# Input projection of a hybrid decoder layer: split weights are kept in DRAM by the second block of tokens and loaded by later ones

## The chip, the cores and the metric

The kernel runs on one core of a Trainium2 chip. The metric is the time of one execution on the device in microseconds, as the median of several runs. A core has a matmul engine (TensorE, PE in the profile; its weight loads are PEld), a vector engine (VectorE, DVE), a scalar engine (ScalarE, ACT), GpSimd (POOL) and a sync engine (SyncE, SP) that here issues every DMA. Each engine works through its own queue of instructions in a fixed order; a semaphore wait at the head of a queue holds all that stands behind it.

## The reference, cut to what matters

One decoder layer over 2048 tokens of width 1024, in float32. The change lies in the first line of it, the combined input projection `h @ w_in` with its 2832 columns:

```python
h = rmsnorm(x, norm_mix[l])
proj = h @ w_in[l]
a_q, a_f, a_i, a_g, b_x, b_g, c_q, c_k, c_v, c_g, c_lr = jnp.split(proj, IN_SPLITS, axis=-1)
o_a = hgrn2_mixer(a_q, a_f, a_i, a_g, lb[l], hgrn_norm[l])
o_b = rglru_mixer(b_x, b_g, ...)
o_c = gla_mixer(c_q, c_k, c_v, c_g, c_lr, ...)
x = x + jnp.concatenate([o_a, o_b, o_c], axis=-1) @ w_out[l]
...                                   # gated MLP with a width-3 convolution, final norm
```

## The kernel before

**Two-part products.** A float32 product is made of three matmuls: every operand is split into a high part (rounded to the matmul's own format, float32r) and a low part (the rest), and `mm3` (L134) adds high x high, high x low and low x high. `split` (L110) makes both parts: a copy into the high part (L106 on ACT, L108 on DVE) and a subtraction into the low part (L113). For weights this is done in `load_w` (L115): a load of raw weights into a tile `wr` (pool `wraw`, three buffers), then the split into `wh` and `wl` (pool `wsp`, three buffers of each), 128 partitions x up to 1024 columns. A table `W_SPLIT` (L38) says for each kind of weights which engine makes which part, and how far ahead of its place the split is put in the order:

```python
W_SPLIT = {"z": ("vector", "vector", 320), "cv": ("scalar", "vector", 0), "qk": ("vector", "vector", 20),
           "ai": ("scalar", "vector", 80), "g": ("scalar", "vector", 160), "bg": ("scalar", "vector", 320),
           "bi": ("vector", "gpsimd", 320), ...}
```

**Blocks of tokens.** The tokens are worked on in four blocks of 512 (`b` = 0 to 3). For each block `in_steps` (L243) lists the steps of the projection for the head groups A and C: two columns blocks `z`, the value weights `cv` (three tiles of weights that all four 128-token steps use) , four `qk`, the `ai` weights (two tiles), four `g`. One column block is `proj` (L185): `load_w`, then 8 x 3 = 24 matmuls of 512 columns. Weights are loaded and split anew for every block. The projection of block `b + 1` is merged, step by step, with the mixing of block `b` (`mix_steps`, L347), which is many small instructions on DVE, ACT, POOL and PE; this is set out at L694 to L712.

**B columns.** For the last block the eight columns blocks of head group B (`s_bg`, L333, kind `bg`) are projected beside its mixing, and the results go to DRAM (`bg_d`). For blocks 0 to 2 the same eight column blocks are projected later, in the B stage (`b_in`, L740, kind `bi`), from `hT`, the turned and split activations, that were kept in DRAM (`h_d`). There each block's `b_in` stands ahead of its `b_mix` (the gated recurrence, mostly DVE) and of `b_out` of the block before (the output projection, with loads of `xr` and stores to `x2_d`). The first `b_in` is put in the order beside the last block's mixing.

**Order.** A scheduler at build time orders each engine's instructions by their place in the program, shifted by `high_priority`, and by when their inputs are expected; buffers are given out as they come free. After about 960 us only the MLP is left, which the change doesn't touch.

Of the kernel before, what the change touches and what calls it, by code (L numbers as in the profile page):

```python
# [8 lines left out]
F32 = mybir.dt.float32  # L9
F32R = mybir.dt.float32r  # L10
I32 = mybir.dt.int32
AF = mybir.ActivationFunctionType
# [4 lines left out]
P = 128  # L17
D = 1024
KT = D // P
# [14 lines left out]
A_Q, A_F, A_I, A_G, B_X, B_G, C_Q, C_K, C_V, C_G, C_LR = (  # L34
    0, 256, 512, 768, 1024, 1536, 2048, 2176, 2304, 2560, 2816)
# [9 lines left out]
def kernel(ctx: ExitStack, tc: tile.TileContext, x, norm_mix, w_in, hgrn_lower_bounds, hgrn_norm,  # L45
# [4 lines left out]
    vec, act, pool, pe, sync = nc.vector, nc.scalar, nc.gpsimd, nc.tensor, nc.sync  # L50
    x, out, w_in, w_out = x[0], out[0], w_in[0], w_out[0]
# [4 lines left out]
    def pool_at(stack, nbytes, name, bufs, **kw):  # L56

        stack.enter_context(tc.tile_pool(name="pad_" + name, bufs=1, **kw)).tile([P, nbytes // 4], F32, name="pad")
        return stack.enter_context(tc.tile_pool(name=name, bufs=bufs, **kw))
# [3 lines left out]
    wsp = pool_at(ctx, 320, "wsp", 3)  # L63
# [5 lines left out]
    dram = ctx.enter_context(tc.tile_pool(name="dram", bufs=1, space=DRAM))  # L69
# [16 lines left out]
    def mm_bank():  # L86
        return bank("mm", 4)

    def aux_bank():
        return bank("aux", 2)  # L90
# [13 lines left out]
    def copy(eng, o, i):  # L104
        if eng is act:
            act.activation(o, i, AF.Copy)  # L106
        else:
            eng.tensor_copy(o, i)  # L108

    def split(raw, hi, lo, e_hi=act, e_lo=vec):  # L110

        copy(e_hi, hi, raw)
        e_lo.tensor_tensor(lo, raw, hi.bitcast(F32), op=ALU.subtract)  # L113

    def load_w(src, n1, n2, tag, tail=None, wpool=None, wcols=D):  # L115

        def part(pool_, dt, nm):
            return pool_.tile([P, wcols], dt, name=nm, tag=nm)[:, :n1 * n2].rearrange("p (a b) -> p a b", b=n2)
        hl = [part(wpool or wsp, F32R, "wh"), part(wpool or wsp, F32R, "wl")]
        raw = part(wraw, F32, "wr")  # L120
        if tail is None:
            sync.dma_start(out=raw, in_=src)
        else:
            m = src.shape[-1]
            sync.dma_start(out=raw[:, :, :m], in_=src)
            sync.dma_start(out=raw[:, :, m:], in_=tail)
        e_hi, e_lo, ahead = W_SPLIT[tag]
        with tc.high_priority(offset=ahead):
            split(raw, hl[0], hl[1], getattr(nc, e_hi), getattr(nc, e_lo))
        return hl  # L130

    w_in_v = w_in.rearrange("(kt p) c -> p kt c", p=P)
# [46 lines left out]
    def proj_mm(w, hT):  # L179
        o = mm_bank()  # L180
        for kt in range(KT):
            mm3(o, [a[:, kt, :] for a in w], [a[:, kt, :] for a in hT], kt == 0, kt == KT - 1)
        return o

    def proj(hT, col, tag):  # L185

        return proj_mm(load_w(w_in_v[:, :, col:col + P], KT, P, tag), hT)

    def merged(a, b):

# [38 lines left out]
    with ExitStack() as cx:  # L229
# [13 lines left out]
        def in_steps(b, B):  # L243
            steps = []
            blk = blks[b % 2]


            def s_z(c):
                if c == 0:
                    B["K"] = blk.tile([P, 3, TB], F32, name="K")  # L250
                    B["L"] = blk.tile([P, 3, TB], F32, name="L")
                copy(vec, B["K"][:, c, :], proj(B["hT"], A_F + c * P, "z"))
            for c in range(2):
                steps.append(lambda c=c: s_z(c))


            def s_vw(col, n):
                if n > 256:
                    B["V"] = blk.tile([P, NTK, 528], F32, name="V")
                B["kn"] = 3 if n > 256 else 4  # L260
                B["ws"] = []
                for k0 in range(0, KT, B["kn"]):
                    ks = slice(k0, min(k0 + B["kn"], KT))
                    B["ws"].append(load_w(w_in_v[:, ks, col:col + 256], ks.stop - k0, n, "cv" if n > 256 else "ai",
                                          w_in_v[:, ks, C_LR:C_LR + 16] if n > 256 else None))

            def s_v(n, at, t):
                o = mm_bank()
                for kt in range(KT):
                    mm3(o[:, :n], [a[:, kt, t * P:(t + 1) * P] for a in B["hT"]],  # L270
                        [a[:, kt % B["kn"], :] for a in B["ws"][kt // B["kn"]]], kt == 0, kt == KT - 1)
                copy(vec, B["V"][:, t, at:at + n], o[:, :n])

            def s_gate():
                V, K, L = B["V"], B["K"], B["L"]
                lr = tmp.tile([16, TB], F32, name="lr", tag="X")
                pt = aux_bank()
                for t in range(NTK):  # L280
                    pe.transpose(out=pt[:16, t * P:(t + 1) * P], in_=V[:, t, 512:528], identity=ident)
                vec.tensor_copy(lr, pt[:16, :])
                gl = aux_bank()
                pe.matmul(gl, gup, lr, start=True, stop=True)
                e, u1 = t2(), t2()
                f = tmp.tile([P, 2, TB], F32, name="f", tag="f", bufs=1)
                z, l01, mn = K[:, 0:2, :], L[:, 0:2, :], L[:, 2, :]
                act.activation(e, gl, AF.Abs, bias=pc["bg"])
                act.activation(e, e, AF.Exp, scale=-1.0)
                act.activation(f, z, AF.Sigmoid)  # L290
                act.activation(z, z, AF.Sigmoid, scale=-1.0)
                vec.tensor_scalar(mn, gl, pc["bg"], 0.0, op0=ALU.add, op1=ALU.min)
                vec.tensor_scalar(u1, e, 1.0, None, op0=ALU.add)
                vec.scalar_tensor_tensor(e, u1, -1.0, e, op0=ALU.add, op1=ALU.subtract)
                for c in range(2):
                    vec.tensor_scalar(f[:, c, :], f[:, c, :], lb1[:, c:c + 1], lb[:, c:c + 1],
                                      op0=ALU.mult, op1=ALU.add)
                vec.tensor_scalar(l01, f, LN_MIN, None, op0=ALU.max)
                vec.tensor_scalar(f, f, F_FLOOR, LN_MIN, op0=ALU.max, op1=ALU.min)
                act.activation(u1, u1, AF.Ln)  # L300
                act.activation(l01, l01, AF.Ln)
                act.activation(f, f, AF.Ln, scale=LN_UP)
                if run.get("out"):
                    run.pop("out")()
                vec.tensor_tensor(e, e, u1, op=ALU.subtract)
                vec.tensor_tensor(mn, mn, e, op=ALU.add)
                vec.tensor_scalar(mn, mn, 1.0 / 16.0, None, op0=ALU.mult)
                vec.scalar_tensor_tensor(l01, f, lnc, l01, op0=ALU.subtract, op1=ALU.add)
                for c in range(2):
                    vec.tensor_scalar(K[:, c, :], K[:, c, :], lb1[:, c:c + 1], None, op0=ALU.mult)  # L310
            for t in range(NTK):
                steps.append(lambda t=t: (s_vw(C_V, 272) if t == 0 and b > 0 else None, s_v(272, 256, t)))
            steps.append(s_gate)


            def s_qk(nm, c, col, scale):
                if nm not in B:
                    B[nm] = blk.tile([P, 3, TB], F32, name=nm)
                act.activation(B[nm][:, c, :], proj(B["hT"], col, "qk"), AF.Copy, scale=scale)
            for nm, c, col, scale in (("Q", 0, A_Q, 1.0), ("Q", 1, A_Q + P, 1.0), ("Q", 2, C_Q, C_SCALE),  # L320
                                      ("K", 2, C_K, 1.0)):
                steps.append(lambda a=(nm, c, col, scale): s_qk(*a))
            for t in range(NTK):
                steps.append(lambda t=t: (s_vw(A_I, 256) if t == 0 else None, s_v(256, 0, t)))


            def s_g(k):
                g = t2()
                copy(vec, g, proj(B["hT"], (A_G, C_G)[k // 2] + (k % 2) * P, "g"))
                sync.dma_start(out=g_d[b][k], in_=g)  # L330


            def s_bg(k):  # L333
                g = t2()
                copy(act, g, proj(B["hT"], (B_X, B_G)[k % 4 // 2] + (k // 4 * 2 + k % 2) * P, "bg"))
                sync.dma_start(out=bg_d[k], in_=g)
            B["load"] = lambda: s_vw(C_V, 272)
            return (steps, [lambda k=k: s_g(k) for k in range(4)],
                    [lambda k=k: s_bg(k) for k in range(8)] if b == NB - 1 else [])

# [217 lines left out]
        for gi, group in enumerate((rows, frows)):  # L558
            n = sum(r[2] for r in group)
# [86 lines left out]
        for b in LEVELS[:5]:  # L646
            n = 64 // b
# [667 lines left out]
```

## Time and profile before

| | us |
|---|---|
| median of 3 runs | 2220.92 |
| lowest and highest | 2212.77, 2224.83 |
| profiled execution, its own time | 2215.95 |
| span of the profiled execution | 2214.2 |

The profile is one execution. Engine times are busy times, of which several can run at once. A matmul's end is modelled, so PE's busy share is an upper bound of how full it is; how dense it works is read from how far apart matmuls start. The page counts 321.41 MB moved by DMA, 145 GB/s on average, nearly all through one queue (SP's).

### The profile page before, as it was taken

The page shows a single profiled execution, that of the slowest core. Times are in us where ns is not written, and L with a number is a line of the kernel's source. Part 1 is how long each engine was busy: PE and PEld are TensorE (multiplying, and loading weights), DVE is VectorE, ACT ScalarE, POOL GpSimd, SP SyncE. Part 2 cuts the span into 40 slices and gives each one's busy share as a digit, 9 for nine tenths or more (in the row PEclk, how much of TensorE's full clock was granted, in tenths as well). Part 3 has the DMA queues.
Part 4 walks back from the last instruction along what each step waited for, and adds up shares of the span by engine and source line. Part 5 has one row for each costly group of instructions (what it writes and reads, how often), then busy time and mean ns, then how long its engine had stood idle before and what let it go on. Part 6 is the DMA issues. An engine that isn't in the chain of part 4 may idle for free.

```text
span 2214.2 us, 31440 instructions
## 1 busy us (share of the span) xinstructions
PE 2142.7 (97%) x12118; PEld 1761.8 (80%) x12118; DVE 1678.8 (76%) x2366; ACT 987.5 (45%) x1361; POOL 349.3 (16%) x456
## 2 busy tenths in 40 slices
PE   7999999999899999999999999999999999999998
PEld 6887778777667878988888887788888887888886
DVE  7799998988768778786676766666666678679676
ACT  3453535433156467454444445544444455226332
POOL 2232341516333231000000000000000000000000
PEclk9999999999999999999999999999999999999999
DMA  7352432345144736643342435522222258667653
GB/s 260 116 180 73 162 97 65 96 148 184 60 136 176 225 121 190 202 136 119 110 134 87 133 95 182 190 80 86 86 86 86 85 176 276 209 205 254 217 174 111
DMA packets 313699, 321.41 MB, mean 145 GB/s; under 512 B 17347, under 2 KB 267214, under 8 KB 312014
## 3 DMA queue, kind: packets, MB, share of 16 engines
q1 hardware_dynamic: 313550, 319.41, 44.5%
q8 instruction: 95, 1.56, 0.3%
q14 instruction: 54, 0.44, 0.1%
HBM read 233.38 MB, written 85.98 MB: 144 GB/s over the span
## 4 chain that ended last, share of the span: by engine, by line
PE 54%; DVE 7%; DMA 5%; ACT 2%; issue 2%; POOL 0%; SPq 0%; DVEq 0%; POOLq 0%; ACTq 0%
PE mm L1072 26%; PE sc L1072 13%; PE aux L1072 6%; PE sc L137 2%; PE sc L138 2%; PE sc L136 2%; DVE wl L113 1%; DMA x_d<-xr 1%; PE mm L138 1%; PE mm L136 1%; PE mm L137 1%; DMA xt<-x_d 1%; DVE xc L801 1%; DMA y<-ps_d 1%; PE mm L913 1%
## 5 line engine op out<-in xcount | busy, mean ns | idle before, releaser
L106 ACT ACTIVATE wh<-wr 128x1024 fp32r<-128x1024 f32 (+3 forms) x217 | 200.8, 928 | 354.6 <-PE mm L1072 91.2
L113 DVE TENSOR_TENSOR wl<-wr,wh 128x1024 fp32r<-128x1024 f32 (+2 forms) x241 | 260.8, 1085 | 102.5 <-ACT wh L106 98.3
L106 ACT ACTIVATE wh<-s 128x1024 fp32r<-128x1024 f32 x116 | 123.0, 1062 | 251.7 <-PE sc L1072 197.8
L138 PE MATMUL mm<-hTh,wl 128*128 128x512 f32 x576 | 231.0, 401 | 2.8 <-POOL wl L113 2.4
L136 PE MATMUL mm<-hTh,wh 128*128 128x512 f32 x576 | 233.6, 406 | 0.0
L137 PE MATMUL mm<-hTl,wh 128*128 128x512 f32 x576 | 231.7, 402 | 0.0
L404 POOL TENSOR_TENSOR qc<-Q,X 32x128 f32<-32x128 f32 x224 | 151.0, 674 | 247.3 <-ACT X L390 116.4
L1072 PE MATMUL mm<-t34h,wh 128*128 128x512 f32 x464 | 181.1, 390 | 1.3 <-DVE y L1238 0.9
L1072 PE MATMUL mm<-t34h,wl 128*128 128x512 f32 x464 | 180.6, 389 | 0.0
L1072 PE MATMUL mm<-t34l,wh 128*128 128x512 f32 x464 | 180.5, 389 | 0.0
L113 DVE TENSOR_TENSOR wl<-s,wh 128x1024 fp32r<-128x1024 f32 x116 | 141.4, 1221 | 18.5 <-ACT wh L106 18.4
L137 PE MATMUL sc<-wl,oh 128*128 128x256 f32 x512 | 146.8, 287 | 2.4 <-DVE wl L113 2.4
L136 PE MATMUL sc<-wh,oh 128*128 128x256 f32 x512 | 146.3, 287 | 0.2 <-DVE xr L834 0.2
L138 PE MATMUL sc<-wh,ol 128*128 128x256 f32 x512 | 145.4, 284 | 0.0
L138 PEld LDWEIGHTS mm<-hTh,wl 128*128 128x128 f32 x576 | 108.6, 189 | 31.1 <-issue 4.3
L136 PEld LDWEIGHTS mm<-hTh,wh 128*128 128x128 f32 x576 | 108.4, 188 | 28.9 <-issue 6.8
L137 PEld LDWEIGHTS mm<-hTl,wh 128*128 128x128 f32 x576 | 108.7, 189 | 27.8 <-issue 7.3
L1141 DVE SCALAR_TENSOR_TENSOR ga<-gr,pcol,ga 128x1024 f32<-128x1024 f32 x84 | 107.6, 1281 | 0.4 <-issue 0.3
L1072 PEld LDWEIGHTS mm<-t34h,wh 128*128 128x128 f32 x464 | 87.1, 188 | 21.2 <-issue 1.7
L137 PEld LDWEIGHTS sc<-wl,oh 128*128 128x128 f32 x512 | 97.5, 190 | 5.8 <-DVE wl L113 3.0
L1072 PEld LDWEIGHTS mm<-t34h,wl 128*128 128x128 f32 x464 | 87.1, 188 | 18.2
L1072 PEld LDWEIGHTS mm<-t34l,wh 128*128 128x128 f32 x464 | 87.1, 188 | 17.9
(335 smaller groups left out, 5508.4 us busy)
## 6 DMA issues: line engine op xcount, KB each, us to landing
wr<-in_w_in_dram SPq DMA_DIRECT2D x80, 512.0 KB
wr<-in_ffn_w_gate_dram SPq DMA_DIRECT2D x42, 512.0 KB
wr<-in_ffn_w_val_dram SPq DMA_DIRECT2D x42, 512.0 KB
wr<-in_w_out_dram SPq DMA_DIRECT2D x32, 512.0 KB
gr_d<-v SPq DMA_DIRECT2D x32, 512.0 KB
ps_d<-y SPq DMA_DIRECT2D x32, 512.0 KB
wr<-gr_d SPq DMA_DIRECT2D x32, 512.0 KB
wr<-in_ffn_w_down_dram SPq DMA_DIRECT2D x25, 512.0 KB
```

The costliest lines, as they stand in the source:

```text
L106: act.activation(o, i, AF.Copy)
L113: e_lo.tensor_tensor(lo, raw, hi.bitcast(F32), op=ALU.subtract)
L136: pe.matmul(o, lh, rh, start=first, stop=False)
L137: pe.matmul(o, lh, rl, start=False, stop=False)
L138: pe.matmul(o, ll, rh, start=False, stop=last)
L404: pool.tensor_tensor(qc[p_, h, :].rearrange("p (n s) -> p n s", s=lev), qo[p_, 2], xo[p_, 2], op=ALU.mult)
L801: vec.tensor_tensor_scan(xc[:, i, :], r[:, i, :], th[:, i, :], initial=hs0[:, c:c + 1], op0=ALU.mult, op1=ALU.add)
L913: pe.transpose(out=pt[:, k * P:(k + 1) * P], in_=xt[:, (k0 + k) * P:(k0 + k + 1) * P], identity=ident)
L1072: pe.matmul(o, lhs[a], rhs[b], start=first and k == 0 and i == 0, stop=last and k == KH - 1 and i == 2, skip_group_check=True)
L1141: vec.scalar_tensor_tensor(ga, gr[:, k:k + TH], pc[f"fw{k}"][:, f:f + 1], ga, op0=ALU.mult, op1=ALU.add)
```

## The change

`load_w` gets a key. The first call with a key that is to be kept loads and splits as before and then stores both parts to two DRAM tiles; a later call with the same key loads the two parts straight into `wh` and `wl`, without `wr` and without a split. Block 0 neither stores nor finds anything (`keep` is `b > 0`), block 1 stores all its 15 weight tiles (30 stores), blocks 2 and 3 load them (60 loads instead of 30). In the last block the eight `bg` calls store (16 stores), and the 24 `bi` calls of blocks 0 to 2 find the same columns (48 loads instead of 24). Two unused arguments go. The loads and stores of parts are issued by SP at their place in the program; the rows of a part tile in DRAM are 4 KB long for 1024 columns, those of the raw weights 512 or 1024 bytes.

```diff
-    def load_w(src, n1, n2, tag, tail=None, wpool=None, wcols=D):
+    parts_d = {}
+
+    def load_w(src, n1, n2, tag, tail=None, key=None, keep=True):
...
-        hl = [part(wpool or wsp, F32R, "wh"), part(wpool or wsp, F32R, "wl")]
+        hl = [part(wsp, F32R, "wh"), part(wsp, F32R, "wl")]
+        if key in parts_d:
+            for a, d in zip(hl, parts_d[key]):
+                sync.dma_start(out=a.bitcast(F32), in_=d)
+            return hl
         raw = part(wraw, F32, "wr")
...
             split(raw, hl[0], hl[1], getattr(nc, e_hi), getattr(nc, e_lo))
+        if key is not None and keep:
+            parts_d[key] = [dram.tile([P, n1, n2], F32, name=f"w_{tag}{len(parts_d)}_{i}") for i in range(2)]
+            for a, d in zip(hl, parts_d[key]):
+                sync.dma_start(out=d, in_=a.bitcast(F32))
         return hl
...
-    def proj(hT, col, tag):
+    def proj(hT, col, tag, keep=True):
 
-        return proj_mm(load_w(w_in_v[:, :, col:col + P], KT, P, tag), hT)
+        return proj_mm(load_w(w_in_v[:, :, col:col + P], KT, P, tag, key=col, keep=keep), hT)
...
-                copy(vec, B["K"][:, c, :], proj(B["hT"], A_F + c * P, "z"))
+                copy(vec, B["K"][:, c, :], proj(B["hT"], A_F + c * P, "z", b > 0))
...
-                                          w_in_v[:, ks, C_LR:C_LR + 16] if n > 256 else None))
+                                          w_in_v[:, ks, C_LR:C_LR + 16] if n > 256 else None, key=("v", col, k0), keep=b > 0))
...
-                act.activation(B[nm][:, c, :], proj(B["hT"], col, "qk"), AF.Copy, scale=scale)
+                act.activation(B[nm][:, c, :], proj(B["hT"], col, "qk", b > 0), AF.Copy, scale=scale)
...
-                copy(vec, g, proj(B["hT"], (A_G, C_G)[k // 2] + (k % 2) * P, "g"))
+                copy(vec, g, proj(B["hT"], (A_G, C_G)[k // 2] + (k % 2) * P, "g", b > 0))
```

## Rows read from the trace of the kernel before

**Rows 1.** The page's first part: busy time, share of the span, instructions.

```profile
PE 2142.7 (97%) x12118; PEld 1761.8 (80%) x12118; DVE 1678.8 (76%) x2366; ACT 987.5 (45%) x1361; POOL 349.3 (16%) x456
```

**Rows 2.** Table of stretches: length, busy time (instructions) of each engine, clock, DMA.

```profile
core 0: us, PE busy (x) PEld busy (x) DVE busy (x) ACT busy (x) POOL busy (x), PEclk, DMA share, GB/s
...
240.00:360.00 120.00, 113.12 (x1012) 92.58 (x1011) 114.39 (x195) 48.17 (x75) 40.18 (x58) 1.00 0.30 89
360.00:490.00 130.00, 125.80 (x1070) 99.52 (x1068) 115.35 (x201) 59.86 (x85) 38.39 (x56) 1.00 0.31 94
490.00:560.00 70.00, 65.17 (x519) 50.61 (x518) 62.98 (x90) 22.62 (x43) 44.47 (x57) 1.00 0.61 203
560.00:640.00 80.00, 75.80 (x450) 49.96 (x450) 52.95 (x88) 19.29 (x28) 23.40 (x21) 1.00 0.23 68
640.00:800.00 160.00, 149.15 (x786) 123.31 (x785) 128.24 (x129) 88.99 (x104) 60.66 (x37) 0.97 0.55 179
...
960.00:2214.00 1254.00, 1238.01 (x5495) 1020.34 (x5494) 881.90 (x1123) 542.22 (x737) 67.47 (x108) 1.00 0.44 143
```

**Rows 3.** Who waited for whom, 240 to 800 us: total, times, longest.

```profile
DVE wh L108 <- PE mm L137: 12.0, 8, 4.3
...
PE sc L427 <- DVE qa L400: 8.3, 7, 2.8
PE aux L775 <- ACT r L777: 6.0, 2, 4.6
...
PE aux L516 <- DVE hl L113: 3.0, 4, 1.2
PE mm L138 <- POOL wl L113: 2.4, 1, 2.4
```

**Rows 4.** The chain that ended last: start, duration, what; B stage, then MLP.

```profile
668.04 3.35 DVE xc L792
...
672.89 0.74 DVE xc L755
...
676.50 2.81 DVE xc L755
...
683.64 3.35 DVE th L797
...
754.04 2.41 DVE wh L108
...
756.62 4.55 DVE ol L113 x2
...
772.16 1.14 DVE th L797
...
1000.22 2.72 PE mm L1072 x12
```

**Rows 5.** Table of stretches again, two of ten microseconds.

```profile
690.00:700.00 10.00, 5.36 (x20) 3.60 (x19) 9.88 (x14) 8.51 (x11) 1.52 (x3) 0.85 0.17 52
700.00:710.00 10.00, 10.00 (x60) 8.11 (x59) 5.94 (x7) 8.71 (x10) 3.95 (x1) 0.81 0.85 341
```

**Rows 6.** DVE's groups of weight splits, 240 to 490: busy us, mean ns, idle before.

```profile
L113 DVE TENSOR_TENSOR wl<-wr,wh 128x1024 fp32r<-128x1024 f32 x25 | 31.4, 1264 | 2.8 <-ACT wh L106 2.5
...
L108 DVE CAST wh<-wr 128x1024 fp32r<-128x1024 f32 x10 | 7.1, 714 | 1.1 <-PE mm L137 0.6 <-PE mm L138 0.4
...
L113 DVE TENSOR_TENSOR wl<-wr,wh 128x816 fp32r<-128x816 f32 x2 | 2.0, 1000 | 0.0
...
L113 DVE TENSOR_TENSOR wl<-wr,wh 128x544 fp32r<-128x544 f32 x2 | 1.7, 860 | 0.0
```

**Rows 7.** GpSimd's group of weight splits, whole span.

```profile
L113 POOL TENSOR_TENSOR wl<-wr,wh 128x1024 fp32r<-128x1024 f32 x24 | 63.8, 2659 | 107.0 <-DVE wh L108 46.2 <-DMA oa<-o_ac_d 19.9 <-PE mm L138 18.4
```

**Rows 8.** SP's queue, 490 to 560 us: what it waited for.

```profile
SPq L336 <- ACT t L106: 38.3, 7, 9.8
```

**Rows 9.** A 512 KB load in 4 KB rows: SP's issue; DMA share, 294 to 298.

```profile
294.54 0.34 SPq L175 DMA_DIRECT2D wbc<-in_norm_ffn_dram  x1
...
DMA  0000000000000002954998996989963334021000
```

More of the change, by code (lines that the diff above doesn't have):

```diff
@@ L113, in split @@
         e_lo.tensor_tensor(lo, raw, hi.bitcast(F32), op=ALU.subtract)
-    def load_w(src, n1, n2, tag, tail=None, wpool=None, wcols=D):
+    parts_d = {}
+    def load_w(src, n1, n2, tag, tail=None, key=None, keep=True):
         def part(pool_, dt, nm):
-            return pool_.tile([P, wcols], dt, name=nm, tag=nm)[:, :n1 * n2].rearrange("p (a b) -> p a b", b=n2)
-        hl = [part(wpool or wsp, F32R, "wh"), part(wpool or wsp, F32R, "wl")]
+            return pool_.tile([P, D], dt, name=nm, tag=nm)[:, :n1 * n2].rearrange("p (a b) -> p a b", b=n2)
+        hl = [part(wsp, F32R, "wh"), part(wsp, F32R, "wl")]
[3 more added lines that the diff above has]
+            return hl
         raw = part(wraw, F32, "wr")
```

## The prediction

> **What bounds the kernel now.** I read the table of stretches first, then the list of who waited, then the chain of waits, then the groups of split instructions. The page says that TensorE (PE) is busy for 97% of the span [rows 1], and from 960 us to the end it really is dense: 1238 of 1254 us [rows 2], at one 512-column matmul every 2.72/12 = 0.227 us [rows 4]. The change doesn't touch that part. In the input projection the picture is less clean. From 240 to 490 us, when the projection of the third and fourth block of tokens (blocks 2 and 3) runs under the mixing of blocks 1 and 2, VectorE (DVE) is busy 114.4 + 115.3 = 229.7 of 250 us and PE 238.9 [rows 2]. Two engines are both close to full, so what one is spared can only be gained as far as the other has idle time. PE's idle time, stretch by stretch, is 6.9 and 4.2 us (240 to 490), 4.8 and 4.2 (490 to 640) and 10.9 (640 to 800), 31 us together [rows 2]. This is a lower bound of its slack: a matmul is drawn about 0.39 us long and the next starts after 0.227, so a stall under some 0.16 us isn't seen.
>
> Most of what PE waited for there by name comes out of DVE or out of the scalar engine (ACT) behind it: 8.3 us for `qa`, 6.0 for `r`, 3.0 for `hl`, and only 2.4 in the row for the weights' low part [rows 3]. So weights are not what PE lacks; DVE's time is. The chain of waits says the same from 664 to 690 us and from 752 to 785: it consists of DVE instructions end to end, and three kinds of them are stretched. Line 792 took 3.35 us and line 797 3.35 us, where line 797 took 1.14 us undisturbed; line 755 took 2.81 us against 0.74 [rows 4]. Each stretch falls on one of the 24 low-part splits that GpSimd (POOL) does for the B columns, of 2.66 us mean [rows 7].
>
> **The change part by part.**
>
> *Blocks 2 and 3 don't split (removed).* Per block: 2 `z`, 4 `qk`, 2 `ai`, 4 `g` tiles of 1024 columns and three `cv` tiles. On DVE that is, for two blocks, 24 low parts at 1.264 us = 30.3, 12 high parts at 0.714 = 8.6, 4 x 1.000 and 2 x 0.860 for `cv`, in all 44.6 us of its 229.7 [rows 6, 2] (the stretch cuts a little off at either end, so its groups count 25 and 10 instead of 24 and 12). ACT loses 18 high parts too, but at 108 of 250 us [rows 2] it isn't a bound. With 185 us left, DVE falls well below PE; what is late next is PE itself, whose idle time there is 11.1 us [rows 2]. I take 7 us of it; the ends are 0 (PE's order stays as full of small switches as now) and 17 (the unseen stalls go too).
>
> *B columns of blocks 0 to 2 don't split (removed).* 24 high parts on DVE and 24 low parts on POOL, 63.8 us of POOL [rows 7]. Between 490 and 640 us the high parts also hold DVE up, since they stand in its queue and wait for PE to free a weight slot, 12.0 us in 8 waits, the longest 4.3 [rows 3]; the mixing of the last block queues behind them. PE's idle time in this stretch is 9.0 us [rows 2]; I take 4 (0 to 9). From 640 to 800 us I go by the chain: four stretched pieces (668.04, 676.50, 683.64, 756.62) give back 2.2 + 2.1 + 2.2 + 2.3 = 8.8 us (the last, two instructions of 1024 columns, against twice 1.14), the high part at 754.04 goes with 2.4, and six further high parts at some 0.6 with 3.6; together 14.8 us [rows 4]. PE comes next there: 10.9 us idle [rows 2], and it ran at a granted clock of 0.85 and 0.81 of full (part of the time at 1.2 instead of 2.4 GHz) in the ten microseconds in which it was idle for 4.6 us and in the ten behind them [rows 5]. I take 10 (4 to 16).
>
> The Trainium skill, SBUF — State Buffer, section "SBUF: two separate sides", has a rule for the stretched rows: a DVE instruction with two SBUF inputs and a GpSimd instruction hold a shared port pair in turn, each for its whole length. The trace agrees where the two meet (3.35 instead of 1.14 us). By the rule alone up to 24 x 2.66 = 64 us of DVE's time could come back, by the rows the 8.8 us that lay on the chain; I keep the rows, because PE caps it.
>
> *Loads (added).* 30 loads of raw weights in blocks 2 and 3 become 60 part loads, 24 for the B columns become 48. The nearest row is a 512 KB load in 4 KB rows: issued at 294.54, its packets end 3.1 us later, and the digits of the 16 engines' share add up to about 1.3 us [rows 9]. A pair behind one another is then ready some 4.5 us after its issue (estimate from that row). Cover: there are three weight slots, and a column of 24 matmuls takes 24 x 0.227 = 5.4 us on PE [rows 4], so a freed slot has two columns, 10.9 us, before it is needed. That hides 4.5 us. It isn't hidden where one projection takes all slots: `cv` holds three and `ai` two, and the next column now waits for a pair of loads (4.5 us) instead of a split (0.71 + 1.26 = 2.0, raw data being there already). Four such places x 2.5 = 10 us; PE has mixing work beside them, so I charge 5 (0 to 10). The part loads no longer pass through DVE's queue, but they wait on the SP queue for PE; behind them stand the stores of `g_d`, the loads of x and, in the B stage, `xr` and `x2_d`.
>
> *Stores (added).* 30 in block 1 and 16 from the last block's B columns. Each waits on SP for its split, and the next raw load stands behind it; that load needs the same split's end when it reuses a raw slot, so in the main nothing new is waited for. In DMA time 16 x 1.3 = 21 us fall into 490 to 560 us, whose share is 0.61 of 70 us = 43 us [rows 2]; 64 of 70 is nearly full, but it fits. I cost them at nothing; if that cover is gone, it is the second rival's price.
>
> Sum: -7 - 4 - 10 + 5 = -16 us. The profiled execution took 2215.95 us (span 2214.2), 5 below the median of 2220.92; taken from the median, 2220.9 - 16 = **2205 us**. About 0.5%, 11 us, is what a measurement of this kernel can tell from no change.
>
> **The rivals.**
>
> *The weights come late and eat the gain.* All four places cost their 2.5 us in full (10 instead of 5), and the nearly full DMA stretch (64 of 70 us, with 4 MB of `hT` loads inside) delays the first B columns by another 8, some 1.5 us for each of five or six columns. Then -21 + 18 = -3: 2218 us. For it: three slots instead of three plus three raw ones. Against it: 4.5 us against 10.9. The Trainium skill, DMA: Bandwidth & Descriptors, section "Bandwidth", gives 6.15 us for a 1 MB transfer, which speaks against the change: (6.15 - 2.0) x 4 = 17 us (estimate) would take nearly the whole gain, 2217 us. The row of 512 KB has a shorter time per byte, and no run so far shows the pair itself.
>
> *The stores stop the raw loads (slower).* If SP reaches a store before its split is done, the next load waits behind it, and prefetch falls to one column: load 3.1 + high part 0.71 + low part 1.26 [rows 9, 6] + two store issues of 0.34 = 5.8 us per column, against 5.4 on PE. In the 23 columns that store, 0.4 us each is 9 us if DVE takes each split at once; but SP already waits 38.3 us in 7 waits for the copies to `bg_d`, 5.5 each [rows 8], and at half of that per column it is 23 x 2.7 = 62. With the -16 of the rest, 2214 to 2267; in the middle 2240 us. It decides from 16/23 = 0.7 us per column upward. Against it: today's loads wait for the same splits.
>
> *The unseen stalls go as well.* Each gain comes near its upper end, 17 + 7 + 13, and the loads cost 4: -33, 2188 us.
>
> **How the numbers follow.** Forecast 0.50 (own range 2196 to 2211), late weights 0.25, stores that stop loads 0.15, larger gain 0.10. Within 0.5% lie the late weights and a little of the forecast and of the stores' lower end: 0.28. Faster is most of the forecast and the larger gain: 0.57. Slower: 0.15. The range reaches from somewhat under the larger gain, 2184, to 2232, which leaves out the upper half of the slower rival and the gain of all upper ends at once (42 us).
>
> **What would show it.** DVE's busy time in the stretch that answers to 240 to 490 falls by about 45 us and PE's idle time there to some 4; the stretched 3.35 us rows in the B stage are gone, POOL's low parts with them; the chain there is no longer DVE end to end. Late weights would show as PE waiting for a DMA into `wh` or `wl`, by name; stopped loads as SP waiting at the new store lines with PE waiting for a split in block 1 or in the last block's B columns. The prediction is wrong if the order of PE's instructions comes out with more switches between small and large matmuls, which no row of before can tell.

## The result and the profile after

The changed kernel takes 2197.05 us (median; 2195.28 to 2199.61) beside 2222.6 us for the kernel before on the same chip: a ratio of 0.9903, 95% interval 0.9884 to 0.9921, which is 18 to 26 us. The forecast of 2205 us was right in sign and its range held the time. The steps behind it were not all right, and one of the largest was wrong. The profiled span fell from 2214.2 to 2193.5 us, by 20.7 us.

The first part of the page of after (busy time, share, instructions), which answers to [rows 1]:

```profile
PE 2137.9 (97%) x12118; PEld 1763.1 (80%) x12118; DVE 1586.7 (72%) x2300; ACT 974.4 (44%) x1343; POOL 268.9 (12%) x432
```

PE has the same 12118 matmuls. DVE has 66 instructions fewer and 92.1 us less busy time. The removed splits account for 44.6 us (blocks 2 and 3) and 24 high parts for some 18 us; the other 30 us or so are instructions that stayed and became shorter. The table of stretches of after, in the columns of [rows 2]:

```profile
240.00:360.00 120.00, 116.72 (x1019) 95.45 (x1017) 96.26 (x178) 42.81 (x69) 34.66 (x57) 0.99 0.42 145
360.00:490.00 130.00, 126.32 (x1071) 100.73 (x1070) 100.08 (x182) 52.47 (x78) 35.57 (x56) 0.99 0.45 160
490.00:560.00 70.00, 68.79 (x536) 53.77 (x535) 57.47 (x93) 23.34 (x45) 38.30 (x56) 1.00 0.85 311
560.00:640.00 80.00, 77.85 (x461) 51.95 (x460) 39.35 (x77) 26.66 (x37) 3.93 (x12) 1.00 0.39 135
640.00:800.00 160.00, 153.04 (x853) 128.79 (x852) 102.53 (x124) 93.27 (x108) 17.25 (x27) 0.99 0.67 226
```

Beside [rows 2], DVE falls from 229.7 to 196.3 us between 240 and 490, but PE's idle time only from 11.1 to 7.0. Between 490 and 640 it falls from 9.0 to 3.4, and between 640 and 800 from 10.9 to 7.0.

Busy shares don't say where time was saved, because the same work lies at another time. Stores and loads that stand at fixed points of the program do. The SP queue's rows of before (start, duration, line, tiles): the stores of the mixing of blocks 1, 2 and 3, the first load of `hT` in the B stage, and the first store of the MLP:

```profile
403.88 0.37 SPq L519 DMA_DIRECT2D o_ac_d<-O  x1
...
545.42 0.37 SPq L519 DMA_DIRECT2D o_ac_d<-O  x1
...
637.21 0.36 SPq L519 DMA_DIRECT2D o_ac_d<-O  x1
...
700.95 0.50 SPq L737 DMA_DIRECT2D hTh<-h_d  x1
...
995.98 0.50 SPq L1146 DMA_DIRECT2D gx_d<-v  x1
```

The same five of after:

```profile
400.46 0.37 SPq L530 DMA_DIRECT2D o_ac_d<-O  x1
...
542.48 0.37 SPq L530 DMA_DIRECT2D o_ac_d<-O  x1
...
624.38 0.41 SPq L530 DMA_DIRECT2D o_ac_d<-O  x1
...
683.19 0.46 SPq L748 DMA_DIRECT2D hTh<-h_d  x1
...
980.11 0.50 SPq L1157 DMA_DIRECT2D gx_d<-v  x1
```

So after is ahead by 3.4, 2.9, 12.8, 17.8 and 15.9 us. Hardly anything is won while blocks 2 and 3 load their weights instead of splitting them; 9.9 us are won between the last two mixing stores, while the B columns run, 4.9 more up to the `hT` load, and 1.9 are given back up to the MLP. The last 4.8 of the 20.7 us appear in the MLP, which the change doesn't touch. From its first store to the end it takes 1218.2 us before and 1213.4 after; in the kernels below, with the same MLP, it takes 1210.3 to 1218.7, so 4.8 us lie within the spread of single executions. Whether the change has a part in them isn't shown: by the medians the gain is 18 to 26 us, so 2 to 10 us of it have no place in these points, which come from one execution each.

DVE's groups in the B stage (last numbers: busy us, mean ns | idle before) show the shorter instructions. Before:

```profile
L755 DVE SCALAR_TENSOR_TENSOR xc<-xb,pcol,xc 128x512 f32<-128x512 f32 x48 | 42.2, 891 | 0.6
L792 DVE SCALAR_TENSOR_TENSOR xc<-gi,xc 128x1024 f32<-128x1024 f32 x8 | 12.0, 1498 | 3.1 <-ACT gi L777 3.1
```

After:

```profile
L766 DVE SCALAR_TENSOR_TENSOR xc<-xb,pcol,xc 128x512 f32<-128x512 f32 x48 | 35.3, 747 | 0.7
L803 DVE SCALAR_TENSOR_TENSOR xc<-gi,xc 128x1024 f32<-128x1024 f32 x8 | 9.8, 1222 | 10.7 <-ACT gi L788 10.7
```

The means 891 and 1498 ns mixed stretched and undisturbed instructions ([rows 4] has 2.81 beside 0.74 us); 747 and 1222 ns are undisturbed ones alone. The ten microseconds in which PE stood idle for 4.6 us in [rows 5] are full, at the full clock. They hold later work now; the work of [rows 5] lies some 18 us earlier, and there, from 680 to 690 us, PE is idle for 1.7 us, also at the full clock. The same place as in [rows 5]:

```profile
690.00:700.00 10.00, 10.00 (x86) 10.00 (x85) 5.79 (x8) 8.43 (x9) 0.00 (x0) 1.00 0.86 329
```

### The profile page after: what moved, and what is told of

Read it like the earlier page. It is cut to its first block, busy times and chain, and to the rows that moved or that the text cites. A ratio compares the mean times of both kernels' runs of the same rounds, so it can differ in the third digit from the quotient of the medians.

```text
span 2193.5 us, 31444 instructions
## 1 busy us (share of the span) xinstructions
PE 2137.9 (97%) x12118; PEld 1763.1 (80%) x12118; DVE 1586.7 (72%) x2300; ACT 974.4 (44%) x1343; POOL 268.9 (12%) x432
## 4 chain that ended last, share of the span: by engine, by line
PE 49%; DMA 3%; DVE 2%; ACT 1%; issue 1%; POOL 0%; SPq 0%; DVEq 0%; POOLq 0%; ACTq 0%
PE mm L1083 26%; PE sc L1083 13%; PE aux L1083 6%; DMA y<-ps_d 1%; DVE wl L113 1%; PE mm L147 1%; PE mm L149 1%; PE mm L148 1%; DVE y L1235 0%; DMA wr<-gr_d 0%; PE mm L924 0%; ACT wh L106 0%; DMA y<-x_d 0%; DMA y<-in_ffn_w_down_dram 0%; DMA hr<-hb_t 0%
## 5 line engine op out<-in xcount | busy, mean ns | idle before, releaser
L106 ACT ACTIVATE wh<-wr 128x1024 fp32r<-128x1024 f32 (+2 forms) x199 | 184.2, 927 | 342.3 <-PE mm L1083 92.0
L113 DVE TENSOR_TENSOR wl<-wr,wh 128x1024 fp32r<-128x1024 f32 (+2 forms) x211 | 225.0, 1069 | 102.9 <-ACT wh L106 98.9
L415 POOL TENSOR_TENSOR qc<-Q,X 32x128 f32<-32x128 f32 x224 | 144.5, 645 | 265.8 <-ACT X L401 122.1
L113 DVE TENSOR_TENSOR wl<-s,wh 128x1024 fp32r<-128x1024 f32 x116 | 141.5, 1222 | 18.9 <-ACT wh L106 18.9
L1083 PEld LDWEIGHTS mm<-t34l,wh 128*128 128x128 f32 x464 | 87.1, 188 | 17.8
```

What stands on the lines that cost most here:

```text
L415: pool.tensor_tensor(qc[p_, h, :].rearrange("p (n s) -> p n s", s=lev), qo[p_, 2], xo[p_, 2], op=ALU.mult)
L1083: pe.matmul(o, lhs[a], rhs[b], start=first and k == 0 and i == 0, stop=last and k == KH - 1 and i == 2, skip_group_check=True)
```

## The experiments

**Repeat.** The changed kernel itself, once more, beside the next two kernels.

> The changed kernel once more, beside the partial ones below on the same chip. Expected 25 us under the kernel before (ratio 0.989), with 480 us of the span reached within 2 us of before, about 15 us gained between 480 and the MLP, and up to 4 us in the MLP, where the first profile had no stretch at half clock at 1383 and 1414 us. If that last part was chance it is 0 here.

Measured: 2192.51 us, 0.9882 [0.9864, 0.9901]. The gain repeats; its size differs between the two measurements by some 0.2%. In its trace the `hT` load that stands at 482.93 us before stands at 480.97, and the MLP starts 16.9 us earlier (979.06), as expected. The MLP itself took 1210.3 us, 7.9 less than in the trace of before, where 0 was expected if the first difference was chance; so the part of the MLP stays open.

**Which half carries the gain.** First the B columns alone, with nothing kept for blocks 2 and 3:

```diff
-    copy(vec, B["K"][:, c, :], proj(B["hT"], A_F + c * P, "z", b > 0))
+    copy(vec, B["K"][:, c, :], proj(B["hT"], A_F + c * P, "z", False))
...
```
(and `False` in the same way for `cv`/`ai`, `qk` and `g`)

> Only the B columns are kept and loaded; blocks 1 to 3 split all their other weights as before. Theory 1 (PE already bounds the projection of blocks 2 and 3, the gain is made by the B columns): 15 us or more under the kernel before, nearly all of the gain. Theory 2 (the 45 us of DVE time spared in blocks 2 and 3 carry a good part, as in the forecast, 7 of 21): 10 us or less under before.

Measured: 2199.64 us, 0.9913 [0.9897, 0.9929]. Nearly the whole gain; the mixing store of block 3 stands at 625.71 us and the `hT` load at 685.57, close to after's 624.38 and 683.19.

Then the other half, with nothing kept of the last block's B columns:

```diff
-    copy(act, g, proj(B["hT"], (B_X, B_G)[k % 4 // 2] + (k // 4 * 2 + k % 2) * P, "bg"))
+    copy(act, g, proj(B["hT"], (B_X, B_G)[k % 4 // 2] + (k // 4 * 2 + k % 2) * P, "bg", False))
```

> Only blocks 1 to 3 keep and load; the B columns are split as before. Theory 1: within 3 us of the kernel before, although DVE has 34 us less to do between 240 and 490 us. Theory 2: 7 us or more under before.

Measured: 2196.7 us, 0.9907 [0.9888, 0.9926], the whole gain again. The edit did less than its expectation says: the B stage still kept its columns, so its block 0 split and stored them and its blocks 1 and 2 loaded them. Only 8 of the 24 GpSimd splits remained. The kernel says nothing of blocks 2 and 3 alone. The clean form also takes the keeping out of the B stage:

```diff
-    copy(act, xb[:, 3:], proj(B["hT"], B_X + c * P, "bi"))
+    copy(act, xb[:, 3:], proj(B["hT"], B_X + c * P, "bi", False))
...
-    copy(act, gb[:, i, :], proj(B["hT"], B_G + (2 * p2 + i) * P, "bi"))
+    copy(act, gb[:, i, :], proj(B["hT"], B_G + (2 * p2 + i) * P, "bi", False))
```

> As blocks_only was meant: blocks 1 to 3 keep and load, and all 24 B columns of the B stage are split from raw weights (in blocks_only the B columns of blocks 1 and 2 were still loaded, from parts stored by block 0's B stage, since their key was left in). Theory 1 (PE bounds the projection of blocks 2 and 3, and the gain is made by the B columns): within 4 us of the kernel before. Theory 2 (DVE's relief in blocks 2 and 3 carries a good part): 7 us or more under before.

Measured: 2214.88 us, 0.999 [0.9978, 1.0003]. Blocks 2 and 3, with 30 splits turned into loads, are worth some 0.2% at most. Yet their stretches look just like after's. Table of stretches of this kernel:

```profile
240.00:360.00 120.00, 116.72 (x1020) 95.47 (x1018) 96.28 (x178) 42.63 (x69) 34.69 (x57) 0.99 0.42 145
360.00:490.00 130.00, 126.31 (x1071) 100.76 (x1070) 100.08 (x182) 52.42 (x78) 35.47 (x56) 0.99 0.40 142
```

DVE is relieved by the same 33 us, and hardly any of it arrives: the mixing stores of blocks 2 and 3 stand at 544.00 and 636.75 us, 1.4 and 0.5 us ahead of before. Its list of waits, 240 to 480 us (total, times, longest), shows where it goes:

```profile
DVE t L108 <- PE mm L149: 9.5, 3, 4.7
```

Before:

```profile
DVE t L108 <- PE mm L138: 0.6, 1, 0.6
```

DVE now waits for PE. The stores by themselves were measured with every later block splitting as before:

```diff
-        if key in parts_d:
+        if False:
...
-        if key is not None and keep:
+        if key is not None and keep and key not in parts_d:
```

> All 46 stores are made, but nothing is loaded back: every block splits as before. If stores cost nothing (they wait for the same splits as the next raw loads): within 3 us of the kernel before. If a store that stands in the SP queue before its split is done holds up the next raw load, as in the slower rival: 9 us over before, up to 60.

Measured: 2217.69 us, 1.0006 [0.9991, 1.0021]. The stores cost nothing that can be seen in the median (1 us, with an interval from -2 to 5). The trace, a single execution, has the mixing stores of blocks 2 and 3 and the start of the MLP 4.0, 6.2 and 5.8 us behind before, with a granted clock of 0.83 from 540 to 580 us. The points in the queue can thus be off by several microseconds where the medians agree.

**What of the B columns it is.** For these columns the change takes three things away: 24 high parts from DVE, their waits in DVE's queue, and 24 low parts from GpSimd. The next two kernels give each engine its work back, on top of the change; the loaded parts stay in use and the result of the added instruction goes nowhere.

```diff
+            if tag == "bi":
+                dummy = part(wraw, F32, "wr")
+                with tc.high_priority(offset=320):
+                    pool.tensor_tensor(dummy, hl[0].bitcast(F32), hl[1].bitcast(F32), op=ALU.subtract)
```

> The changed kernel with one more instruction per loaded B column: GpSimd subtracts the two loaded parts into a tile that nobody reads, 128 x 1024 as in the old split, 24 times. DVE's share of the old split stays away. If the gain of the B stage comes from the stretched DVE instructions beside GpSimd's splits: the 3.4 us rows come back and 8 to 15 of the 25 us are lost again. If it comes from DVE's own high parts and their waits: 3 us or less are lost.

Measured: 2218.05 us, 1.0007 [0.9994, 1.0019]. One GpSimd subtraction per column, which nobody needs, takes the whole gain, more than the 8 to 15 us that were expected. Its page's first part, then GpSimd's group and one of DVE's:

```profile
PE 2140.9 (97%) x12118; PEld 1762.8 (80%) x12118; DVE 1624.1 (73%) x2300; ACT 973.1 (44%) x1343; POOL 338.1 (15%) x456
...
L129 POOL TENSOR_TENSOR wr<-wh,wl 128x1024 f32<-128x1024 f32 x24 | 67.3, 2805 | 88.2 <-DMA wl<-w_bg 58.6 <-DMA wh<-w_bg 22.9 <-issue 2.6
...
L770 DVE SCALAR_TENSOR_TENSOR xc<-xb,pcol,xc 128x512 f32<-128x512 f32 x48 | 43.6, 921 | 0.7
```

DVE has exactly after's 2300 instructions and yet 37.4 us more busy time (1624.1 against 1586.7); the mean of the group is 921 ns (before 891, after 747). One meeting, in the timeline of this kernel:

```profile
678.46 2.74 POOL L129 TENSOR_TENSOR wr<-wh,wl 128x1024 f32<-128x1024 f32 x1
...
678.87 2.88 DVE L824 SCALAR_TENSOR_TENSOR gs<-oa,pcol,gs 128x512 f32<-128x512 f32 x1
...
682.34 0.74 DVE L824 SCALAR_TENSOR_TENSOR gs<-oa,pcol,gs 128x512 f32<-128x512 f32 x1
```

The DVE instruction starts 0.41 us behind GpSimd's, and ends 0.55 us behind its end; alone it takes 0.74. Its length fits a wait for the end of GpSimd's instruction, drawn as busy (0.55 us is somewhat less than 0.74, but ends on GpSimd are rough in the profile). What follows in the SP queue, with the mixing store of block 3 and the `hT` load:

```profile
630.09 0.41 SPq L534 DMA_DIRECT2D o_ac_d<-O  x1
...
702.05 0.46 SPq L752 DMA_DIRECT2D hTh<-h_d  x1
```

That is 5.7 and 18.9 us later than after; the MLP starts at 999.44 us, 19.3 later. The control gives DVE an instruction for each column instead, on the same loaded tile:

```diff
-                    pool.tensor_tensor(dummy, hl[0].bitcast(F32), hl[1].bitcast(F32), op=ALU.subtract)
+                    vec.tensor_copy(dummy, hl[0].bitcast(F32))
```

> The changed kernel with a copy on DVE per loaded B column into a tile that nobody reads, 128 x 1024 as the old high part, 24 times; nothing on GpSimd. If GpSimd is the cause: 5 us or less are lost (24 x 0.7 = 17 us of DVE time, a third of it on the chain). If DVE's high parts and their place in its queue are the cause: 10 us or more.

Measured: 2188.34 us, 0.9892 [0.9875, 0.9908]. The 24 copies took 16.5 us of DVE's time (686 ns each), about that of the high parts that the change removed, and cost nothing; 48 instructions of the `xc` group stay at 747 ns. They too read the loaded part, and in the kernel with the subtraction PE waits for a loaded part only once between 490 and 980 us, for 0.5 us. So a weight slot that is held longer isn't what cost the time there.

The other way round, in the kernel before: high parts from DVE to ACT, GpSimd's low parts left.

```diff
-           "bi": ("vector", "gpsimd", 320),
+           "bi": ("scalar", "gpsimd", 320),
```

> The kernel before, with the high part of the B columns made by ACT instead of DVE; GpSimd still makes the low parts. If DVE's high parts, which wait in its queue for a weight slot (12 us), cost much: 5 us or more under the kernel before. If GpSimd's low parts are the cause: within 4 us of it.

Measured: 2212.88 us, 0.9989 [0.998, 0.9997], about 2 us. The 12.0 us that DVE's high parts waited for PE in [rows 3] were cheap. Two groups of this kernel show what remains:

```profile
L113 POOL TENSOR_TENSOR wl<-wr,wh 128x1024 fp32r<-128x1024 f32 x24 | 61.6, 2567 | 104.4 <-ACT wh L106 104.4
...
L755 DVE SCALAR_TENSOR_TENSOR xc<-xb,pcol,xc 128x512 f32<-128x512 f32 x48 | 43.7, 924 | 0.7
```

**Busy GpSimd, or GpSimd that reads.** The same place and nearly the same GpSimd time, but instructions that only write (a copy of one element per partition ties them to the load):

```diff
-                    pool.tensor_tensor(dummy, hl[0].bitcast(F32), hl[1].bitcast(F32), op=ALU.subtract)
+                    pool.tensor_copy(dummy[:, 0, 0:1], hl[1][:, 0, 0:1].bitcast(F32))
+                    for _ in range(3):
+                        pool.memset(dummy, 0.0)
```

> As pool_back, but GpSimd's extra work per loaded B column is three memsets of 128 x 1024 (0.95 us each in the trace) behind a copy of one column, about as long as the old low part's 2.66 us, and reading next to nothing. If the loss of pool_back came from the length of GpSimd's queue (its small copies for the convolution's carry stand behind): again some 25 us lost. If it came from DVE being held while GpSimd reads two tiles: 8 us or less lost, and no stretched DVE rows.

Measured: 2198.1 us, 0.9914 [0.9889, 0.9939]: the gain is kept but for a few microseconds at most. Its first page part and the two groups:

```profile
PE 2134.2 (98%) x12118; PEld 1760.5 (80%) x12118; DVE 1591.0 (73%) x2300; ACT 973.0 (44%) x1343; POOL 343.4 (16%) x528
...
L131 POOL MEMSET wr<- 128x1024 f32 x72 | 69.1, 959 | 3.5
...
L772 DVE SCALAR_TENSOR_TENSOR xc<-xb,pcol,xc 128x512 f32<-128x512 f32 x48 | 35.2, 744 | 0.7
```

GpSimd spends 69.1 us on them, as much as on the subtractions, and DVE's instructions aren't stretched (the longest of these 48 took 753 ns). So it is not a busy GpSimd that holds DVE, and not an order of the queues, but GpSimd instructions that read. All 24 read two tiles; whether one would do wasn't tried.

**The gain without DRAM.** In the kernel before, the two splits of a B column on ACT and DVE; nothing stored, nothing loaded in parts:

```diff
-           "bi": ("vector", "gpsimd", 320),
+           "bi": ("scalar", "vector", 320),
```

> The kernel before with the B columns' high parts on ACT and low parts on DVE, so that GpSimd splits nothing; no part goes through DRAM. Beside bi_act_pool only the low parts move. If GpSimd's splits are the whole price: 12 to 22 us under the kernel before, although DVE takes over 24 x 1.22 = 29 us. If the loads from DRAM are needed because DVE has no room: 5 us or less.

Measured: 2194.54 us, 0.9904 [0.9882, 0.9926], the same as the whole change. DVE gets 24 low parts for 24 high ones, 13.2 us more by [rows 6], and its busy time nevertheless falls from 1678.8 to 1652.1. The mixing store of block 3 stands at 632.35 us and the MLP starts at 973.81: 5.0 us are won between the last two mixing stores and 17.3 behind them. The group at line 755 of this kernel:

```profile
L755 DVE SCALAR_TENSOR_TENSOR xc<-xb,pcol,xc 128x512 f32<-128x512 f32 x48 | 35.4, 745 | 0.8
```

**Why blocks 2 and 3 gave next to nothing.** The counterpart of relieving DVE is to relieve PE. In the kernel before, the products with the low part of the weights are left out for `qk` in blocks 2 and 3, 64 matmuls of 512 columns, 14.5 us of PE:

```diff
-            mm3(o, [a[:, kt, :] for a in w], [a[:, kt, :] for a in hT], kt == 0, kt == KT - 1)
+            (mm2 if less else mm3)(o, [a[:, kt, :] for a in w], [a[:, kt, :] for a in hT], kt == 0, kt == KT - 1)
...
-    act.activation(B[nm][:, c, :], proj(B["hT"], col, "qk"), AF.Copy, scale=scale)
+    act.activation(B[nm][:, c, :], proj(B["hT"], col, "qk", b > 1), AF.Copy, scale=scale)
```

> The kernel before without the low x high products of the qk columns in blocks 2 and 3 (this part of the projection is left out): 64 matmuls of 0.227 us, 14.5 us of PE time; DVE has as much to do as before. With blocks_clean, where DVE had 45 us less to do and nothing was gained, this asks whether PE is the bound there: then 480 us of the span is reached 10 to 14 us earlier. If both share the bound: 5 us or less.

Measured: 2211.69 us, 0.9982 [0.9966, 0.9998]: about 4 of the 14.5 us arrive. PE's waits, 240 to 480 us, in this kernel:

```profile
PE mm L135 <- DVE wh L108: 7.3, 2, 4.0
...
PE sc L431 <- DVE qa L404: 4.5, 5, 2.2
```

The first row is new; the second stood at 4.7 us in before. With PE relieved, PE waits for DVE; with DVE relieved, DVE waits for PE. I read this as a stretch that is bound by both at once. Relieving both together wasn't tried, so that this would pay is argued and not shown.

**Late weights, made to happen.** On top of the change, the parts of `w_out` are kept too; two of them are wanted together:

```diff
-                    ws = [load_w(w_out_v[:, k0:k0 + 4, cols], 4, 256, "out") for k0 in (0, 4)]
+                    ws = [load_w(w_out_v[:, k0:k0 + 4, cols], 4, 256, "out", key=("o", qd, k0)) for k0 in (0, 4)]
```

> The changed kernel with the output projection's weights kept too: block 0 splits and stores its eight pairs of parts, blocks 1 to 3 load them. 24 high parts less on ACT (25 us) and 24 low parts less on DVE (29 us) in the B stage. If DVE is still on the chain there: 5 to 10 us under the changed kernel. If PE bounds it now: within 4 us of it; if three weight slots are too few, since each pair takes two: slower.

Measured: 2212.12 us, 0.9983 [0.9968, 0.9998], which gives back most of the gain. PE's waits, 640 to 980 us, in this kernel:

```profile
PE sc L147 <- DMA wh<-w_out: 8.8, 8, 2.3
...
PE sc L148 <- DMA wl<-w_out: 3.1, 3, 1.2
```

This is the first rival in the place where it holds: slots are taken in pairs, PE waits 11.9 us by name for parts, the MLP starts 17.0 us later than after (997.13), and less for DVE to do (1562.8 us) is of no use.

## Why the prediction was right, and where not

The sum was -16 us: -7, -4, -10 and +5. By the five points in the SP queue the changed kernel starts its MLP 15.9 us earlier. The sum agrees with that point and lies a little under the 18 to 26 us of the medians, but all four of its terms were mis-sized, and the errors cancelled: -2.9, -9.9, -3.0 and 0 were measured in this trace. That the sum came out so close was luck.

*Blocks 2 and 3 (-7): wrong.* DVE fell by 33 us where 45 were announced (by 39.4 over the whole span when only these blocks are changed), and PE's idle time to 7.0 us where 4 were. By itself this half is worth 0.999 [0.9978, 1.0003]. The step that failed is "what is late next is PE itself, whose idle time there is 11.1 us": that idle time was taken as what DVE costs. The kernel with less PE work, where about 4 of 14.5 us arrived, fits PE and DVE handing the bound to each other in this stretch: each relief alone brought a few microseconds at most. The measured value lies near the low end of this term's range, 0.

*B columns, 490 to 640 us (-4): mechanism wrong and too small.* The points in the queue give -9.9 there, outside the range of this term. I had put it down to the high parts in DVE's queue. Moved to ACT they bring 0.9989, and put back on DVE as copies they cost nothing. About half of it is the low parts on GpSimd: from the mixing store of block 2 to that of block 3 it takes 91.8 us before, 81.9 after, 87.4 with the subtraction back and 86.8 with the splits moved off GpSimd. What brings the other half, 4 to 5 us, isn't shown. Between 490 and 640 I had not looked for stretched instructions.

*B stage, 640 to 800 us (-10): right mechanism, size not settled.* The stretched rows were found in the chain and put down to GpSimd's 24 low parts, and that holds: subtraction back, gain gone (1.0007). From block 3's mixing store to the MLP the change brings -3.0 us net (-4.9 to the `hT` load, then +1.9), which is below the range of this term, but moving the splits off GpSimd brings -17.3 there, above it. On which side of the mixing store a gain shows differs from kernel to kernel, so the two terms can only be held against the runs together: -14 announced, -12.9 in after, -13.4 with the B columns alone and -22.3 with the splits moved.

The chain was also read incompletely. The prediction counted four stretched pieces; three more stand in the same chain of before, each beside a low part on GpSimd:

```profile
765.51 3.13 DVE th L794
...
773.90 4.48 DVE xc L801 x2
...
783.18 2.21 DVE xc L755
```

The same instructions take 1.13, 2.46 and 0.74 us undisturbed, so these add 5.5 us. The high part at 754.04, counted as 2.4 us of its own, takes 0.60 elsewhere in the chain; the other 1.8 us are a stretch too, beside this one:

```profile
753.79 2.36 POOL L113 TENSOR_TENSOR wl<-wr,wh 128x1024 fp32r<-128x1024 f32 x1 [10.66 <-DVE wh L108]
```

So the chain held 16.1 us of stretches and not 8.8, and the remaining 4.2 us for high parts were no price at all, as the copies on DVE show. Nor was it DVE end to end: between 752 and 785 us 5.6 of its 33 us are GpSimd, ACT and issue. That the chain is no longer DVE's holds for the repeat: between 640 and 800 us three lines of PE's projection matmuls lead it, with 16% each. The chain of after itself can't be followed back beyond 964 us.

The Trainium skill, SBUF — State Buffer, section "SBUF: two separate sides", says that a DVE instruction with two SBUF inputs is shut out for a GpSimd instruction's whole length, and only by one that reads SBUF. Both halves are borne out here: 2.88 instead of 0.74 us beside a subtraction, and no stretch beside memsets of nearly the same total length. In the prediction the rule had a price of up to 64 us of DVE's time, beside 8.8 us by the chain; DVE's time measured 37.4 us with the subtraction back, of which 19.3 reached the MLP. The rule's sentence deserved more weight than four rows of the chain, which shows only the meetings that happened to end last.

*Late loads (+5): not there.* PE waits once for a part, 0.4 us. Its row in the list of waits of after, 240 to 800 us:

```profile
PE mm L148 <- DMA wl<-w_ai: 0.4, 1, 0.4
```

The size of the load was about right: the packets of a pair of 408 KB parts of `cv`, issued at 363.84 us, end some 4 us later, where 4.5 were estimated for 512 KB. The cover of three slots holds at `cv` and `ai` too; that it is PE's mixing work that covers the rest is argued. By the page of the Trainium skill, DMA: Bandwidth & Descriptors, section "Bandwidth", which the prediction set against this, the loads would have cost 17 us; the trace doesn't agree, 0.4 us. The Trainium skill's figure is for loads issued from GpSimd, and these are issued by SP, ahead of their use. The prediction's remark that the row of 512 KB has a shorter time per byte doesn't hold up to its last packet: 3.1 us for 512 KB is 6.2 for 1 MB. The same term becomes real with `w_out`, which costs some 20 us against the change (0.9983 beside 0.9903 and 0.9882).

*Stores (0): right*, 1.0006 alone. Half of the announced sign did show: SP waited 67 us at the new store line. Its queue in after, whole span:

```profile
SPq L140 <- ACT wh L106: 43.9, 8, 15.6
SPq L140 <- DVE wl L113: 23.2, 17, 4.2
```

The other half, PE waiting behind it, didn't: the kernel with the stores alone loses nothing by its median. The DMA share between 490 and 560 us rose from 0.61 to 0.85, where 64 of 70 (0.91) was announced.

*The unseen stalls* didn't come out of blocks 2 and 3. The remaining 4.8 us of the profiled difference lie in the MLP; before's trace has a granted clock of 0.83 there in the ten microseconds from 1380 and from 1410 us, after's has 1.00, and why isn't known.

## What to carry to other kernels

An elementwise instruction with two inputs isn't free on GpSimd, even where GpSimd is idle: look at DVE's mean per group beside its fastest instance, and where the first is larger, look in the timeline for a GpSimd instruction over the long ones. Here 24 such instructions (64 us of GpSimd) cost about 1% of the kernel, and two words in a table of engines won it back as well as a round trip through DRAM did. Where two engines are both nearly full in a stretch, price the relief of one at nothing until the relief of the other has been measured.

## What was not expected of the hardware

A DVE instruction that GpSimd shuts out is drawn as busy, not as waiting: 24 subtractions raised DVE's busy time by 37.4 us without one instruction more, about 1.6 us for each. GpSimd's memsets, 69.1 us against 67.3, raised it by 4.3 us. So a high share of DVE isn't by itself work, and idle time can't show the cause: DVE's group has hardly any before it (0.7 us for 48 instructions). And it isn't only instructions with two inputs that are held: the cast at 754.04 us reads one tile and took 2.41 us instead of 0.60.
